# A norm chain for the first tile, products of zeros in the head, and two state-space parts three k-steps later

## The chip, the cores and the metric

One core of a Trainium2 chip runs the whole step. The metric is the device time of one execution in microseconds (us), as the median of several runs. Its engines are TensorE (PE: matmuls, and PEld for weight loads), VectorE (DVE), ScalarE (ACT), GpSimd (POOL) and SyncE (SP), which only issues transfers here. Each engine executes its own instructions in a fixed order and waits on semaphores for the others.

## The reference

One layer of a streaming encoder over 1024 prompt rows with 16 learned rows ahead of them, and 32 sample rows:

```
xn = rmsnorm(h);  z = xn @ w_in          # q latent | kv latent | rope key | u | g_a | g_b
o_a = attention(z) @ w_o_attn            # latent attention with rotary keys and a chunk mask
s   = gelu(y), y = s5_scan(u)            # 64 groups of 16 channels, 64 complex states each
        # x = f * (B u);  h_t = lam * h_{t-1} + x_t;  y = Re(C h) + D u
o_b = (s @ w_glu_v) * sigmoid(s @ w_glu_g)
h  += (sigmoid(g_a) * o_a + sigmoid(g_b) * o_b) @ w_out
h  += relu(rmsnorm(h) @ w_mlp_up)^2 @ w_mlp_down
```

The outputs are the rows, the new caches and the new states. Everything is float32 at the interface.

## The kernel before

Products run in float32r with both operands split into a high and a low half (`split`, L183 and L186): each 128x128 block is multiplied three times, xh·wh, xl·wh and xh·wl (`lin_part`, L261 to L271, the matmul is L267). ScalarE makes the high half by a copy, VectorE or POOL the low half by a subtraction. For the weights ScalarE makes `wh` and POOL `wl`, one unit ahead of its use.

**Head (L369 to L413).** A string, `HEAD`, lists the steps in order: `g` loads the norm's gains and spreads them over the partitions by two products (L393), `x` loads one of nine row tiles, `i` the identity, `l` and `w` load and split a weight unit, `n` with some digits computes the norm factors of these tiles in one chain (`stat`: a square with a row sum on ScalarE, L357, then ten small operations of `rsqrt` on VectorE), `m` scales a tile (L366), `t` transposes half a tile on TensorE and splits it into `xh` and `xl` (`to_cols`; tile 8 at once), and `p` runs one chunk of 268 columns of the first two weight units. `p00` is the first of these; it needs tiles 0, 1 and 8.

**State-space stage (about 37 to 440 us).** A loop over slots runs one unit of `w_in` in each (`run_unit`): 128 output columns, 8 k-steps of 9 matmuls, three products for three chunks of rows. The first slots compute units of u (chunks of 358 columns), later ones gates and latents (chunks of 396, 396 and 264 columns). These matmuls I call dense. Their PSUM tiles, tag `acc`, are five buffers, and a unit takes three; `finish` has ScalarE copy them to `gst` (L312, L314).

The state-space work comes in eight groups j of 128 channels, each in six parts that are laid over the slots by `START = [2, 4, 7, 9, 12, 15, 17, 20]`: `st0` in slot START[j], `st1` one slot later, `st2` two, `st3` four, `st4` five, `st5` six. A part that is a generator is advanced by one `next()` ahead of each k-step of the slot's unit (L263), so its TensorE work is mixed into the dense unit.

- `st0(j)`: POOL builds a table `tb` of powers by doubling (two memsets and 49 small operations, L554 to L562); VectorE builds `clm` and `wxt` (L419 to L427).
- `st1(j)`: TensorE transposes `wxt` (L584), ScalarE copies the result (L585); then the products `clm`·`bd` (L595) and `ext` (L602).
- `st2(j)`: TensorE computes the scan's input with U and W (L620), ScalarE copies it to `xs` (L626), VectorE multiplies with the table (A, Bt: L641, L642), adds (L643, L644), scans (L647), multiplies again (L649, L650) and forms `hb` (L653, L654). POOL makes the scan's coefficients L (L638 to L640).
- `st3(j)`: for four pairs of channel blocks TensorE multiplies U with M (L671) and adds `hb` times `clm` (L676); ScalarE copies to Y (L682); Y goes to DRAM and comes back as `yt`.
- `st4(j)`: the GELU's inner polynomial: square on ScalarE (L695), a multiply-add on VectorE (L696), `gw` on POOL (L697).
- `st5(j)`: tanh of `gw` on ScalarE (L702), the last product on VectorE (L703), and a store.

`tb` and `wxt` have one buffer each, `clm` two. After the stage come GLU, attention, the output projection and the MLP.

The program is written unit by unit, but the order on each engine is not the order of writing: the framework's scheduler places instructions by a simulated timeline of its own, so a step that is written later can move others that the diff doesn't touch.

Of the kernel before, what the change touches and what calls it, by code (L numbers as in the profile page):

```python
# [10 lines left out]
F32 = mybir.dt.float32  # L11
# [103 lines left out]
KENG = ['vpvpvpp', 'vvpppvv', 'vpvvvvv', 'vpppvpp']  # L115


HEAD = "g x0 x8 x1 i l0 x2 x3 l1 x4 x5 x6 x7 n081 m0 t00 m8 t01 t80 m1 t10 w t11 w p00 p01 n23 m2 t20 t21 m3 t30 t31 p10 p11 n4567 m4 t40 t41 m5 t50 t51 p20 p21 m6 t60 t61 m7 t70 t71 p30 p31"
CH0 = [(0, 268), (268, 268), (536, 268), (804, 268)]
START = [2 + int(2.6 * j) for j in range(8)]  # L120
G3 = [(0, 3), (3, 3), (6, 2)]
# [35 lines left out]
def tile_layer(ctx: ExitStack, tc: tile.TileContext, a: dict, o: list, dbg=None):  # L157
    nc = tc.nc
# [143 lines left out]
    with tc.tile_pool(reuse_waits="tile", name="s5", bufs=1) as sp, tc.tile_pool(reuse_waits="tile", name="sps", bufs=3, space=PSUM) as sps:  # L302
# [6 lines left out]
        def finish(kind, m, M, outs, st):  # L309
            for c0, n, ps in outs:  # L310
                if kind in "ab":
                    nc.scalar.activation(st[:M, c0:c0 + n], ps, AF.Tanh, scale=0.5)  # L312
                else:
                    nc.scalar.activation(st[:M, c0:c0 + n], ps, AF.Copy)  # L314
# [20 lines left out]
        X = {}  # L335
        spare = iter([("M", 2)] * 2 + [("U", 2)] * 2 + [("Y", 3)] * 3 + [("A", 1), ("Bt", 1)])

        def load_x(t):
            tag, bufs = next(spare)
            X[t] = sp.tile([128, D], F32, tag=tag, name="X", bufs=bufs)[:128 if t < 8 else 48]  # L340
            if t < 8:
                nc.sync.dma_start(X[t], x_p[t])
            else:
                nc.sync.dma_start(X[t][0:32], x_s)
                nc.sync.dma_start(X[t][32:48], a["meta_tokens"])
# [18 lines left out]
        def scale(t):  # L364
            R = X[t].shape[0]
            nc.vector.scalar_tensor_tensor(X[t], X[t], rsx[t], gbc[:R], op0=ALU.mult, op1=ALU.mult)  # L366
# [16 lines left out]

        for w in HEAD.split():
            op, i = w[0], [int(c) for c in w[1:]]
            if op == "g":

                grow = sp.tile([1, D + 128], F32, tag="clt", name="grow")
                nc.vector.memset(grow[:, D:], 1.0)
                nc.scalar.dma_start(grow[:, :D], a["norm_mix"])  # L390
                for q in range(2):
                    pt = sps.tile([128, 512], F32, tag="sp", name="sp")
                    nc.tensor.matmul(pt, lhsT=grow[:, D:], rhs=grow[:, 512 * q:512 * q + 512], start=True, stop=True)  # L393
                    nc.scalar.activation(gbc[:, 512 * q:512 * q + 512], pt, AF.Copy)
            elif op == "i":
                nc.sync.dma_start(ident, a["c_ident"])
            elif op == "x":
                load_x(*i)
            elif op == "l":
                ws.load(*i)  # L400
            elif op == "w":
                w01.append(ws.get(split_ahead=False))
            elif op == "n":
                stat(i)
            elif op == "m":
                scale(*i)
            elif op == "t":
                to_cols(*i)
            else:
                finish("u", i[1], 128, lin(gps, "acc", *w01[i[1]], *xfull, 8, 128, [CH0[i[0]]]), st01[i[1]])  # L410
# [3 lines left out]
        with ExitStack() as _:  # L414
# [91 lines left out]

            bb = sp.tile([128, 2, 32, 16], F32, tag="W", name="bb")
            for q, nme in enumerate(("ssm_b_re", "ssm_b_im")):
# [69 lines left out]
            def st1(j):  # L578
                cl, wx = hold[j]["cl"], hold[j]["wx"]
                W = sp.tile([128, 2, 4, 128], F32, tag="W", name="W")  # L580
                for q in range(2):
                    pp = sps.tile([128, 4, 128], F32, tag="sp", name="sp")
                    for g in range(4):
                        nc.tensor.transpose(pp[:, g], wx[:, q, g].rearrange("p a b -> p (a b)"), ident)  # L584
                    nc.scalar.activation(W[:, q], pp, AF.Copy)  # L585
                    yield

                for g2 in range(2):
                    hs = slice(64 * g2, 64 * g2 + 64)
                    for q in range(2):  # L590
                        V.tensor_copy(bd[hs, q, :, g2, :], bbar[hs, q, 4 * j:4 * j + 4])
                pk = sps.tile([128, 512], F32, tag="sp", name="sp")
                for g in range(4):
                    for q in range(2):
                        nc.tensor.matmul(  # L595
                            pk[32 * g:32 * g + 32, 0:128],
                            lhsT=bd[:, q, g].rearrange("p a b -> p (a b)"),
                            rhs=cl[:, q, g, 0:8].rearrange("p a b -> p (a b)"),
                            start=(q == 0), stop=(q == 1), tile_position=(0, 32 * g),
                        )  # L600
                yield
                V.tensor_copy(ext[:, 7:15].rearrange("p a b -> p (a b)"), pk[:, 0:128])  # L602
                V.scalar_tensor_tensor(ext[:, 7], m16, dd[:, j:j + 1], ext[:, 7], op0=ALU.mult, op1=ALU.add)
                nc.sync.dma_start(ext_d[j], ext.rearrange("p a b -> p (a b)"))
                M = sp.tile([128, 8, 128], F32, tag="M", name="M", bufs=2)
                src = ext_d[j].rearrange("(g c) x -> c g x", c=16)
                for s in range(T):
                    nc.sync.dma_start(M[16 * s:16 * s + 16], src[:, :, 16 * (7 - s):16 * (7 - s) + 128])
                hold[j].update(W=W, M=M)

            def st2(j):
                gs = slice(4 * j, 4 * j + 4)
                U, tb, W = hold[j]["U"], hold[j]["tb"], hold[j]["W"]
                G = nc.gpsimd

                for g in range(4):
                    px = sps.tile([128, 512], F32, tag="sp", name="sp")
                    for q in range(2):
                        for g2 in range(2):
                            nc.tensor.matmul(  # L620
                                px[64 * g2:64 * g2 + 64, KC * q:KC * q + KC],
                                lhsT=W[:, q, g, 64 * g2:64 * g2 + 64], rhs=U[:, 2 * g + g2],
                                start=True, stop=True, tile_position=(0, 64 * g2),
# [36 lines left out]
            def st3(j):  # L660
                hj = hold.pop(j)
                U, M, cl, hb = hj["U"], hj["M"], hj["cl"], hj["hb"]
                Y = sp.tile([128, 8, KQ], F32, tag="Y", name="Y", bufs=3)


                for ps_ in ((0, 1, 2), (3,)):
                    py = [sps.tile([128, 512], F32, tag="sp", name="sp") for _ in range(2)]
                    for e, pr in enumerate(ps_):
                        c = slice(e * KQ, (e + 1) * KQ)
                        for b in range(2):  # L670
                            nc.tensor.matmul(py[b][:, c], lhsT=M[:, 2 * pr + b], rhs=U[:, 2 * pr + b, 0:KQ],  # L671
                                             start=True, stop=False)
                        for q in range(2):
                            for b in range(2):
                                hs = slice(64 * b, 64 * b + 64)
                                nc.tensor.matmul(  # L676
                                    py[b][:, c], lhsT=cl[hs, q, pr, 1:9].rearrange("p a b -> p (a b)"),
                                    rhs=hb[hs, q, pr], start=False, stop=(q == 1),
                                )
                        yield  # L680
                    for b in range(2):
                        nc.scalar.activation(  # L682
                            Y[:, 2 * ps_[0] + b:2 * ps_[-1] + b + 1:2],
                            py[b][:, :len(ps_) * KQ].rearrange("p (g k) -> p g k", k=KQ), AF.Copy
                        )
                for g in range(8):
                    nc.sync.dma_start(y_d[j][16 * g:16 * g + 16].rearrange("c (t k) -> t c k", t=T), Y[:, g])
                yt = sp.tile([128, NQT], F32, tag="Y", name="yt", bufs=3)
                nc.sync.dma_start(yt, y_d[j])
                hold[j] = dict(yt=yt)  # L690

            def st4(j):
                yt = hold[j]["yt"]
                w = sp.tile([128, NQT], F32, tag="Y", name="gw", bufs=3)
                nc.scalar.activation(w, yt, AF.Square)  # L695
# [694 lines left out]
    with tc.tile_pool(reuse_waits="tile", name="mg", bufs=1) as mg:  # L1390
# [23 lines left out]
        for m in range(8):  # L1414
# [3 lines left out]
            for q in range(2):  # L1418
# [3 lines left out]
                pt = tpp.tile([128, 4, 128], F32, tag="tp", name="tp")  # L1422
# [5 lines left out]
            pt = tpp.tile([128, 512], F32, tag="tp", name="tp")  # L1428
# [21 lines left out]
    pt = tpp.tile([128, 512], F32, tag="tp", name="tp")  # L1450
# [8 lines left out]
    for g in range(3):  # L1459
        pt = tpp.tile([128, 512], F32, tag="tp", name="tp")  # L1460
        b = blk[4 * g:4 * g + 4]
        for c0, n in b:
            i = c0 // 128
            nc.tensor.matmul(pt[:, c0 - 512 * g:c0 - 512 * g + n], lhsT=y[:n, i:i + 1].to_broadcast([n, 128]),
                             rhs=ident[:n, :n], start=True, stop=True)
        w = sum(n for _, n in b)
# [109 lines left out]
```

## Time and profile before

| | us |
|---|---|
| median of 3 runs (2079.85 to 2081.4) | 2080.04 |
| the profiled execution | 2084.05 |
| its span | 2082.3 |
| TensorE busy | 2027.0 |
| VectorE busy | 1109.3 |
| ScalarE busy | 727.5 |
| POOL busy | 681.2 |

The mean granted clock of TensorE is 0.992 of full speed; full is 2.4 GHz, and the only other level is 1.2. A page of the profile shows one execution: busy times are sums of instruction durations, and the span runs from the first to the last instruction. In the timelines a number in square brackets is the time that the engine sat idle right before, with the instruction that released it.

### The profile page before, as it was taken

How to read it: one execution, taken by the hardware profiler on the slowest of the kernel's cores; microseconds unless marked ns; L12 is line 12 of the kernel's file. 1: busy time of each engine (PE TensorE's matmuls, PEld its weight loads, DVE VectorE, ACT ScalarE, POOL GpSimd, SP SyncE). 2: the span in 40 equal slices, each digit the busy share in tenths (PEclk: the TensorE clock that was granted, in tenths of full speed). 3: DMA queues.
4: the chain of work that ended last, by engine and by line, in shares of the span. 5: the costliest groups of instructions: out<-in, count | busy, mean ns of one | idle time of the engine just before them, and what ended most of it. 6: DMA issues, size and time to landing. Idle time of an engine off the chain costs nothing.

```text
span 2082.3 us, 34103 instructions
## 1 busy us (share of the span) xinstructions
PE 2027.0 (97%) x12943; PEld 1923.2 (92%) x12943; DVE 1109.3 (53%) x3048; ACT 727.5 (35%) x1738; POOL 681.2 (33%) x916
## 2 busy tenths in 40 slices
PE   6999999999999899999999999999999999999999
PEld 6988888899999788888888999999999999999999
DVE  5969776534575688888885544432222222222222
ACT  4213222223332567676755223321222212122222
POOL 0577776621222334233444211112121221212121
PEclk9999999999999999999999999999999999999999
DMA  5334434435444101110114434411111121211113
GB/s 144 113 109 124 137 117 143 134 119 173 134 129 129 44 5 28 17 28 17 26 23 132 150 119 125 171 31 56 36 51 50 37 58 35 61 31 56 41 41 104
DMA packets 256177, 170.70 MB, mean 82 GB/s; under 512 B 63240, under 2 KB 239453, under 8 KB 256014
## 3 DMA queue, kind: packets, MB, share of 16 engines
q1 hardware_dynamic: 256012, 168.53, 27.7%
q8 instruction: 102, 1.67, 0.3%
q14 instruction: 61, 0.50, 0.1%
q10 hardware_dynamic: 2, 0.00, 0.0%
HBM read 124.08 MB, written 44.41 MB: 81 GB/s over the span
## 4 chain that ended last, share of the span: by engine, by line
PE 82%; DVE 12%; DMA 2%; ACT 2%; issue 1%; POOL 0%; SPq 0%; ACTq 0%; DVEq 0%; POOLq 0%
PE acc L267 40%; PE pj L267 22%; PE po L1274 3%; PE pj L1045 3%; PE pj L1105 2%; PE pt L1249 1%; PE sp L676 1%; PE Sp L1192 1%; PE Sp L1184 1%; PE Sp L1187 1%; PE Sp L1185 1%; PE Sp L1186 1%; DVE clt L419 1%; PE sp L620 1%; PE sp L671 1%
## 5 line engine op out<-in xcount | busy, mean ns | idle before, releaser
L186 POOL TENSOR_TENSOR wl<-raw,wh 128x1024 fp32r<-128x1024 f32 (+2 forms) x164 | 331.3, 2021 | 981.8 <-ACT wh L183 971.9
L183 ACT ACTIVATE wh<-raw 128x1024 fp32r<-128x1024 f32 (+2 forms) x166 | 148.8, 896 | 755.9 <-PE acc L267 354.2
L267 PE MATMUL acc<-xh,wh 128*128 128x264 f32 (+6 forms) x736 | 188.9, 337 | 1.8 <-ACT xh L183 1.8
L267 PE MATMUL acc<-xh,wl 128*128 128x264 f32 (+4 forms) x736 | 181.2, 327 | 0.0
L267 PE MATMUL acc<-xl,wh 128*128 128x264 f32 (+5 forms) x736 | 181.0, 327 | 0.0
L267 PEld LDWEIGHTS acc<-xh,wh 128*128 128x128 f32 (+1 forms) x736 | 127.4, 190 | 14.3 <-issue 7.4
L267 PEld LDWEIGHTS acc<-xl,wh 128*128 128x128 f32 (+1 forms) x736 | 129.6, 190 | 2.1 <-issue 0.7
L267 PEld LDWEIGHTS acc<-xh,wl 128*128 128x128 f32 (+1 forms) x736 | 129.7, 190 | 1.8 <-issue 0.7
L1501 DVE TENSOR_TENSOR yacc<-pj,yacc 128x352 f32<-128x352 f32 x96 | 44.5, 518 | 139.5 <-PE pj L267 139.5
L1501 DVE TENSOR_TENSOR yacc<-acc,yacc 128x352 f32<-128x352 f32 (+1 forms) x96 | 44.6, 518 | 113.0 <-PE acc L267 113.0
L186 DVE TENSOR_TENSOR al<-t,ah 128x352 fp32r<-128x352 f32 x96 | 64.7, 700 | 71.6 <-ACT ah L183 71.6
L267 PE MATMUL acc<-sh,wh 128*128 128x352 f32 x384 | 93.0, 325 | 1.0 <-ACT sh L751 1.0
L267 PE MATMUL acc<-sl,wh 128*128 128x352 f32 x384 | 93.6, 324 | 0.0
L267 PE MATMUL acc<-sh,wl 128*128 128x352 f32 x384 | 92.9, 324 | 0.0
L1483 DVE SCALAR_TENSOR_TENSOR t<-acc,rstd 128x352 f32<-128x352 f32 x48 | 23.5, 518 | 117.9 <-PE acc L267 117.9
L267 PE MATMUL acc<-ah,wl 128*128 128x352 f32 (+1 forms) x384 | 85.2, 324 | 0.0
L267 PE MATMUL pj<-al,wh 128*128 128x352 f32 x384 | 84.6, 324 | 0.0
L267 PE MATMUL pj<-ah,wh 128*128 128x352 f32 x384 | 84.3, 323 | 0.0
L267 PE MATMUL acc<-al,wh 128*128 128x352 f32 (+1 forms) x384 | 84.1, 323 | 0.0
L267 PE MATMUL acc<-ah,wh 128*128 128x352 f32 (+1 forms) x384 | 84.0, 323 | 0.0
L267 PE MATMUL pj<-ah,wl 128*128 128x352 f32 x384 | 84.0, 323 | 0.0
L267 PE MATMUL acc<-ha,wh 128*128 128x352 f32 x360 | 77.5, 323 | 4.1 <-ACT mh__13991 L183 4.1
(468 smaller groups left out, 5388.6 us busy)
## 6 DMA issues: line engine op xcount, KB each, us to landing
raw<-in_w_mlp_up_dram SPq DMA_DIRECT2D x32, 512.0 KB
raw<-in_w_mlp_down_dram SPq DMA_DIRECT2D x64, 256.0 KB
raw<-in_w_in_dram SPq DMA_DIRECT2D x29, 512.0 KB
ud<-gst SPq DMA_DIRECT2D x8, 536.0 KB
U<-ud SPq DMA_DIRECT2D x64, 67.0 KB
yd<-Y SPq DMA_DIRECT2D x64, 66.0 KB
yt<-yd SPq DMA_DIRECT2D x8, 528.0 KB
sd<-gw SPq DMA_DIRECT2D x8, 528.0 KB
```

The source lines that it names most:

```text
L183: nc.scalar.activation(hi, src, AF.Copy)
L186: lo_eng.tensor_tensor(lo, src, hi.bitcast(F32), ALU.subtract)
L267: nc.tensor.matmul(pt[:M, :n], lhsT=w[:, k, :], rhs=x(k, c0, n), start=(k == 0 and p == 0), stop=(k == kt - 1 and p == 2),)
L419: eng.tensor_tensor(t1, ar, br, ALU.mult)
L620: nc.tensor.matmul(px[64 * g2:64 * g2 + 64, KC * q:KC * q + KC], lhsT=W[:, q, g, 64 * g2:64 * g2 + 64], rhs=U[:, 2 * g + g2], start=True, ...
L671: nc.tensor.matmul(py[b][:, c], lhsT=M[:, 2 * pr + b], rhs=U[:, 2 * pr + b, 0:KQ], start=True, stop=False)
L676: nc.tensor.matmul(py[b][:, c], lhsT=cl[hs, q, pr, 1:9].rearrange("p a b -> p (a b)"), rhs=hb[hs, q, pr], start=False, stop=(q == 1),)
L1045: nc.tensor.matmul(ps[:R], lhsT=x[:, c, k0:k0 + R], rhs=w[:, c, :], start=(c == 0 and q == 0), stop=(c == 1 and q == 2))
L1105: nc.tensor.matmul(ps[:R, :384], lhsT=x[:, c, 128 * i:128 * i + R], rhs=w[:, c, :], start=(c == 0 and q == 0), stop=(c == 2 and q == 2))
L1274: nc.tensor.matmul(po[:, :256], lhsT=w, rhs=x, start=st["first"], stop=(last and q == len(grp) - 1))
L1483: nc.vector.scalar_tensor_tensor(t, ps, 0.0, rstd[:, c], op0=ALU.max, op1=ALU.mult)
L1501: nc.vector.tensor_tensor(yacc[:, m, c], ps, yacc[:, m, c], ALU.add)
```

## The change

Three edits.

1. In the head tile 0 has a norm chain of its own, and is scaled and transposed ahead of tiles 8 and 1, which share one. The identity's load is issued before x1's.
2. After the gain products a tile `zero` is set to zero on VectorE, and five products of 512 columns of it go to a PSUM tile that nothing reads. `zero` uses the buffer of `tb`, which is not yet in use.
3. `st1` and `st3` begin with three empty yields, so their work starts three k-steps later in the unit that they are mixed into.

```diff
-HEAD = "g x0 x8 x1 i l0 x2 x3 l1 x4 x5 x6 x7 n081 m0 t00 m8 t01 t80 m1 t10 w t11 w p00 p01 n23 m2 ...
+HEAD = "g x0 x8 i x1 l0 x2 x3 l1 x4 x5 x6 x7 n0 m0 t00 t01 n81 m8 m1 t80 w t10 t11 w p00 p01 n23 m2 ...
...
                     nc.scalar.activation(gbc[:, 512 * q:512 * q + 512], pt, AF.Copy)
+
+                zero = sp.tile([128, 1088], F32, tag="tb", name="zero")
+                nc.vector.memset(zero, 0.0)
+                pt = sps.tile([128, 512], F32, tag="sp", name="sp")
+                for q in range(5):
+                    nc.tensor.matmul(pt, lhsT=zero[:, 0:128], rhs=zero[:, 0:512], start=(q == 0), stop=(q == 4))
...
             def st1(j):
                 cl, wx = hold[j]["cl"], hold[j]["wx"]
                 W = sp.tile([128, 2, 4, 128], F32, tag="W", name="W")
+                for _ in range(3):
+                    yield
...
                 Y = sp.tile([128, 8, KQ], F32, tag="Y", name="Y", bufs=3)
+                for _ in range(3):
+                    yield
```

Lines of the changed kernel lie 6 higher than those named above from L395 on, 8 higher behind `st1`'s yields, 10 higher behind `st3`'s.

**TensorE in slot 6**, where `st3(0)` and `st2(1)` are mixed into a unit of u. Before, the first products with M and `hb` stand ahead of the unit's first matmul:

```order
L267 MATMUL acc<-xh,wl 128x356
L671 MATMUL sp<-U,M 128x132 x2
L676 MATMUL sp<-hb,clm 128x132 x4
L620 MATMUL sp<-U,W 64x134 x4
L267 MATMUL acc<-xh,wh 128x358 x2
```

Now it begins with the scan's input, and so it goes on:

```order
L628 MATMUL sp<-U,W 64x134 x4
L267 MATMUL acc<-xh,wh 128x358 x2
L267 MATMUL acc<-xl,wh 128x358 x2
L267 MATMUL acc<-xh,wl 128x358 x2
L628 MATMUL sp<-U,W 64x134 x4
```

The first use of `hb` moved behind 27 dense matmuls and 12 of the scan's input.

**VectorE around the polynomial of `st4(0)`** (L696 before, L706 now). Before, it stands between the two scans of group 1:

```order
L647 SCALAR_TENSOR_TENSOR Gs<-L,A 128x544
L696 TENSOR_SCALAR gw<-gw 128x1056
L647 SCALAR_TENSOR_TENSOR Gs<-L,A 128x544
L419 TENSOR_TENSOR clt<-pw,bbar 128x128
L420 TENSOR_TENSOR clt<-pw,bbar 128x128
L421 TENSOR_TENSOR wxt<-clt 128x8x16 x3
L649 TENSOR_TENSOR A<-Gs,tb 128x1088
L650 TENSOR_TENSOR Bt<-Gs,tb 128x1088
```

Now it comes after that group's `hb` and after `clm` of group 2:

```order
L661 TENSOR_TENSOR hb<-A,Bt 128x4x128
L662 TENSOR_TENSOR hb<-A,Bt 128x4x128
L661 TENSOR_TENSOR hb<-A,Bt 128x4x4
L662 TENSOR_TENSOR hb<-A,Bt 128x4x4
L664 TENSOR_TENSOR fin<-A,Bt 128x8
L665 TENSOR_TENSOR fin<-A,Bt 128x8
L431 SCALAR_TENSOR_TENSOR clm<-clt 128x144 x4
L706 TENSOR_SCALAR gw<-gw 128x1056
L425 TENSOR_TENSOR clt<-pw,bbar 128x128
```

The scans and both products with the table moved ahead of it as well.

**POOL from the end of table 1 on.** Before, the weights' `wl` and `gw(0)` follow the table (1233), and the next table (1801) begins behind them:

```order
L427 TENSOR_TENSOR tb_1233<-tt_1234 128x4x3
L186 TENSOR_TENSOR wl_1906<-raw_1607,wh_1905 128x1024
L697 TENSOR_TENSOR gw_1788<-gw_1788,yt_1722 128x1056
L638 COPY L_2360<-mg8_779 128x544
L554 MEMSET tb_1801 128x4
L555 MEMSET tb_1801 128x4
```

Now the next table (1822) begins first:

```order
L433 TENSOR_TENSOR tb_1254<-tt_1255 128x4x3
L646 COPY L_2381<-mg8_800 128x544
L186 TENSOR_TENSOR wl_1927<-raw_1628,wh_1926 128x1024
L647 MEMSET L_2381 128x4
L648 MEMSET L_2381 128x4
L560 MEMSET tb_1822 128x4
L561 MEMSET tb_1822 128x4
```

and `gw(0)` comes 17 operations later:

```order
L428 TENSOR_TENSOR tt_1823<-tb_1822,ek_804 128x4x4
L429 TENSOR_TENSOR tt_1823<-tb_1822,ek_804 128x4x4
L707 TENSOR_TENSOR gw_1809<-gw_1809,yt_1794 128x1056
L433 TENSOR_TENSOR tb_1822<-tt_1823 128x4x4
L425 TENSOR_TENSOR tt_1823<-tb_1822,ek_804 128x4x8
```

The same trade of places happens at tables 4 and 7. ScalarE's order around `tanh(0)` is the same in both: table load, tanh, one `wh`, then the three copies of slot 7's unit to `gst`. On TensorE the third chunk of slot 8's unit comes, in the new order, after two chunks of three k-steps and five products of `st3(1)`.

## Rows read from the trace of the kernel before

**Rows 1.** The page, part 1: busy time, share of the span and instructions of each engine.

```profile
PE 2027.0 (97%) x12943; PEld 1923.2 (92%) x12943; DVE 1109.3 (53%) x3048; ACT 727.5 (35%) x1738; POOL 681.2 (33%) x916
```

**Rows 2.** TensorE's waits by releaser, 0 to 60 us, then 60 to 440 us (total, times, longest).

```profile
PE sp L372 <- DVE X L366: 9.1, 1, 9.1
...
PE sp L584 <- DVE wxt L421: 5.5, 4, 2.2
PE sp L676 <- DVE hb L653: 4.2, 2, 4.0
```

**Rows 3.** Timeline of TensorE, state-space stage: start, duration, operation, [idle before <- releaser].

```profile
133.35 1.25 PE L676 MATMUL sp<-hb,clm 64*128 64x132 f32 x8 [3.98 <-DVE hb L653]
...
169.66 0.33 PE L584 MATMUL sp<-ident,wxt 128*128 128x128 f32 x1 [0.85 <-DVE wxt L421]
...
253.90 0.33 PE L584 MATMUL sp<-ident,wxt 128*128 128x128 f32 x1 [2.21 <-DVE wxt L421]
...
385.62 0.33 PE L584 MATMUL sp<-ident,wxt 128*128 128x128 f32 x1 [1.91 <-DVE wxt L421]
```

**Rows 4.** Windows: us, busy (x) of PE, PEld, DVE, ACT, POOL, PEclk, DMA share, GB/s.

```profile
120.00:140.00 20.00, 16.02 (x94) 14.74 (x94) 13.04 (x22) 2.65 (x7) 12.51 (x37) 0.83 0.23 59
254.40:257.80 3.40, 3.40 (x13) 3.38 (x12) 3.40 (x12) 0.46 (x1) 3.35 (x4) 0.50 0.23 93
21.70:25.70 4.00, 4.00 (x16) 3.77 (x17) 3.51 (x12) 1.45 (x3) 0.00 (x0) 1.00 0.63 64
26.69:28.67 1.98, 1.98 (x18) 1.98 (x17) 1.64 (x11) 0.15 (x1) 0.00 (x0) 1.00 0.22 40
131.40:136.45 5.05, 3.10 (x19) 2.51 (x20) 2.27 (x11) 0.52 (x3) 4.23 (x17) 0.51 0.08 26
169.70:178.26 8.56, 8.51 (x65) 7.55 (x66) 6.92 (x27) 1.60 (x4) 7.88 (x17) 1.00 0.32 128
```

**Rows 5.** Timelines of TensorE and ScalarE in the head, 0 to 36 us.

```profile
2.25 3.75 PE L393 MATMUL sp<-grow 1*128 1x512 f32 x4 [2.25 <-DMA grow<-in_norm_mix_dram]
...
21.68 0.82 PE L267 MATMUL acc<-xh,wh 128*128 128x268 f32 x2 [0.39 <-ACT xh L183]
...
16.29 0.60 ACT L183 ACTIVATE xh<-sp 128x512 fp32r<-128x512 f32 x1 [0.15 <-PE sp L372]
16.78 1.05 ACT L357 ACTIVATE sq<-X 128x1024 f32<-128x1024 f32 x1
```

**Rows 6.** Timeline of TensorE, slots 6 to 8.

```profile
149.16 0.68 PE L620 MATMUL sp<-U,W 128*64 128x134 f32 x8
...
156.11 0.53 PE L267 MATMUL acc<-xh,wh 128*128 128x396 f32 x2
...
167.87 0.61 PE L671 MATMUL sp<-U,M 128*128 128x132 f32 x4
```

**Rows 7.** Timeline of VectorE, slot 7.

```profile
149.27 1.15 DVE L421 TENSOR_TENSOR clm<-clt 128x144 f32<-128x144 f32 x4 [15.57 <-PE sp L676]
...
151.94 1.28 DVE L641 TENSOR_TENSOR A<-xs,tb 128x1088 f32<-128x1088 f32 x1
...
158.06 1.28 DVE L647 TENSOR_TENSOR_SCAN Gs<-L,A 128x544 f32<-128x544 f32 x1
159.26 0.68 DVE L696 TENSOR_SCALAR gw<-gw 128x1056 f32<-128x1056 f32 x1
...
161.06 2.41 DVE L419 TENSOR_TENSOR clt<-pw,bbar 128x128 f32<-128x128 f32 x1
```

**Rows 8.** Timeline of ScalarE, slots 7 and 8.

```profile
165.83 1.09 ACT L702 ACTIVATE gw<-gw 128x1056 f32<-128x1056 f32 x1 [4.13 <-POOL gw L697]
...
168.59 1.15 ACT L312 ACTIVATE gst<-acc 128x396 f32<-128x396 f32 x3
```

**Rows 9.** Timeline of POOL, slots 7 and 8.

```profile
163.29 2.51 POOL L697 TENSOR_TENSOR gw<-gw,yt 128x1056 f32<-128x1056 f32 x1
...
169.71 3.57 POOL L419 TENSOR_TENSOR tt<-tb,ek 128x4 f32<-128x4 f32 x1
```

More of the change, by code (lines that the diff above doesn't have):

```diff
@@ L115 @@
 KENG = ['vpvpvpp', 'vvpppvv', 'vpvvvvv', 'vpppvpp']
-HEAD = "g x0 x8 x1 i l0 x2 x3 l1 x4 x5 x6 x7 n081 m0 t00 m8 t01 t80 m1 t10 w t11 w p00 p01 n23 m2 t20 t21 m3 t30 t31 p10 p11 n4567 m4 t40 t41 m5 t50 t51 p20 p21 m6 t60 t61 m7 t70 t71 p30 p31"
+HEAD = "g x0 x8 i x1 l0 x2 x3 l1 x4 x5 x6 x7 n0 m0 t00 t01 n81 m8 m1 t80 w t10 t11 w p00 p01 n23 m2 t20 t21 m3 t30 t31 p10 p11 n4567 m4 t40 t41 m5 t50 t51 p20 p21 m6 t60 t61 m7 t70 t71 p30 p31"
 CH0 = [(0, 268), (268, 268), (536, 268), (804, 268)]
```

## The prediction

> **What bounds the kernel.** The page's first part comes first: TensorE is busy 97% of the span, VectorE 53% [rows 1], so the bound is TensorE. No edit here takes matmuls out of a busy stretch; it can only remove idle time, or time at the low clock. TensorE's table of waits says where that is: the head, 9.1 us for the first scaled tile, and the state-space stage, 5.5 us on `wxt` in four stalls and 4.2 on `hb` in two between 60 and 440 us [rows 2]. The timeline places them: 3.98 us on `hb` at 133.35 in slot 6, then on `wxt` 0.85 in slot 8, 2.21 in slot 13 and 1.91 in slot 21 [rows 3]; what is left of the sums is 0.5 on `wxt` (slot 3) and 0.2 on `hb` (slot 16). Two are longer than they look. TensorE's clock is granted at 0.83 between 120 and 140 us, and at 0.50 (1.2 GHz) from 254.4 to 257.8, just after the stalls of slots 6 and 13 [rows 4]. At half clock half of the time is lost: 1.7 us at slot 13; at slot 6 the mean of 0.83 over 20 us is 3.4 us, of which I count 2.5, the rest lying in the stall.
>
> So all the state-space stage can give back is 5.5 + 4.2 of waits and 4.2 at the low clock, 13.9 us, 0.7% of the time. One measurement can tell some 0.2%, 4.2 us, from no change.
>
> **The change, part by part.** The sum is made against the profiled execution, 2084.05 us (span 2082.3), 4.0 us over the median of 2080.04; I move the difference to the median.
>
> *Head.* A chain of its own has x0 scaled before x8 and x1 are. It costs VectorE one norm chain more, ten small operations in 1.98 us [rows 4]. But the first product p00, now at 21.68, needs x8 and x1 as well, and on ScalarE one more square (1.06 us, as X4's) stands ahead of the first copy: 16.29 now, 17.4 then [rows 5]. VectorE does all of the old work and one chain more before p00, ScalarE just the old, so p00 stays near 21.7 (21.6 to 22.4), and the scalings of the later tiles move by the added chain at most. I take +0.4, bounds −2 and +1.5.
>
> *Products of zeros.* The memset is one VectorE pass over 1088 columns, 1.28 by the nearest row [rows 7], while VectorE waits for the squares. Two gain products took 3.75 us, so five take 9.4, from 6.0 to 15.4 at worst [rows 5], less if the clock rises on the way. TensorE is idle for 9.1 us there [rows 2], and nothing reads the result. Without this cover x0's transposes would move from 12 to 15.4, still ahead of the copy at 17.4. Cost 0.
>
> By the Trainium skill (TensorE: Matmul & The Clock Gate, "The HAM clock gate") a busy array is granted its full clock and an idle one half, so the zeros would have p00 run at full rate; by that rule p00 would gain some 2 us. The trace agrees that p00 starts slowly behind idle time, though its granted clock is shown as 1.00: 16 products in 4.00 us from 21.7, then 18 in 1.98 [rows 4]. But in the new order too TensorE idles right before p00, from about 15 to 17.4.
>
> *st3 three k-steps later, slot 6.* 27 dense matmuls and 12 of the input projection now stand ahead of the first use of `hb(0)`: 27 × 0.163 (slot 7's 72 products take 156.11 to 167.87) + 12 × 0.17 (eight passes, four products, in 0.68) = 6.4 us [rows 6] against a stall of 3.98. The stall goes, and the low clock after it: −6.5. st1's delay puts 4 × 0.16 or more ahead of the transposes in slot 3: −0.54; the 0.23 of slot 16 goes too. Slot 8's `wxt` stall of 0.85 goes by the 27 matmuls.
>
> *What is late next, slot 8.* With these 7.0 us gone TensorE opens slot 8 at 167.87 − 7.0 = 160.9. Then 18 products of 396 columns, at 0.163 × 396/352 = 0.183, are 3.3 us and five small ones 0.6 [rows 6]: at 164.8 it wants the third column chunk. This chunk's PSUM buffer is the first of slot 7's unit, one of five, and its copy out on ScalarE stands behind `tanh(0)` and one `wh` split, both before and after. Before, tanh ran at 165.83 once POOL's `gw(0)` was done, and the copies at 168.59, in time [rows 8]. Now `gw(0)` is later twice: on VectorE its polynomial stands behind group 1's whole scan part, on POOL behind 17 operations of the next table, which wait for the last reader of `tb(1)`. The chain, with durations from [rows 7 to 9]:
> - POOL's table 1 was ready for VectorE's first product with it at 151.94, and is about 1 us earlier now that less delays POOL's start: the two products, 1.28 each, end near 153.
> - Two sums of half the size 1.3, two scans 2.5: 156.8. Four `clm` 1.1: 157.9. Two products 2.6, one of them held by POOL's `wl` as the small product of 161.06 was (2.41 where its like take 0.29), 2.1: 162.6. This frees POOL's table.
> - VectorE goes on: eight small products and four `clm` at 0.29 are 3.4, `hb` (two of half size) 1.3, then the polynomial 0.7: 168.0.
> - POOL from 162.6: 17 small operations. Undisturbed the same 17 of table 1 took 5.05 us (131.40 to 136.45); beside a busy VectorE the first of table 2 alone was held 3.57, and fifteen of them took 8.56 (the row's 17 count a memset and the next operation) [rows 4, 9]. I take 8.6: 171.2. `gw` 2.5: 173.7.
> - ScalarE: tanh 1.1, `wh` 1.0 (165.83 to 168.59 held both, and a wait of 0.7), first copy 0.4: 176.2.
>
> TensorE waits 164.8 to 176.2, **11.4 us**. Without contention the table is free at 160.5, the 17 operations end at 165.5, the polynomial at 165.9, `gw` at 168.4 and the copy at 170.9: a wait of 6.1. I take 11.4 since the row at 169.71 is the same operation of the same table at the same place beside the same engine. After a wait of that length the low clock comes back; the row of slot 13 prices it at 1.7, that of slot 6 at 2.5: +2.0.
>
> By the Trainium skill (SBUF — State Buffer, "Who interferes with whom") the two engines share one port pair that the later one waits for until the running instruction ends; POOL would then lose one VectorE operation, at most 1.3 us, at its first product, and the wait would be some 2 us less. The row shows 3.57 us, longer than any of VectorE's operations then (0.28 to 1.28).
>
> *Slots 13 and 21.* POOL's order repeats with tables 4 and 7 (`gw(2)` and `gw(5)` behind the next table's first operations). Their start is less sure, so I take the undisturbed 6.1 each, and the low clock of 1.7 for slot 13. Removed are 2.21 + 1.7 and 1.91.
>
> **Sum:** head +0.4; slot 3 −0.5; slot 6 −6.5; slot 8 −0.85 + 11.4 + 2.0 = +12.55; slot 13 6.1 + 1.7 − 3.9 = +3.9; slot 16 −0.2; slot 21 6.1 − 1.9 = +4.2. Together +13.85: 2097.9 for a profiled execution, **2093.9** on the median's footing.
>
> Elsewhere nothing moves: the order after the stage's end is as before. GLU reads what the last parts write, 27 products or 4.4 us later for group 7; the projection units that follow them without state-space parts cover it, and without that cover it costs 4.4.
>
> **Rivals.**
> 1. *No new wait (faster).* Place: the first copy of slot 7's unit on ScalarE. If `gw(0)` leaves POOL before about 162, so that tanh, `wh` and the copy end by 164.8, TensorE never asks in vain, and only the removed stalls count: −0.5 − 6.5 − 0.85 − 3.9 − 0.2 − 1.9 + 0.4 = −13.5, 2066.5; with a wait of a few us at the three places, 2071. For it: ScalarE was in time before, and no row of TensorE's waits in the stage names `gst` [rows 2]. Against: `gw` stands behind a chain that even undisturbed ends at 168.4. Chance 0.25, since a chain of twelve links can be off by its first.
> 2. *Gains and waits cancel (same).* The undisturbed chain: slot 8 −0.85 + 6.1, slots 13 and 21 waiting about as long as they did, slot 6 −6.5, slot 3 −0.5, slot 16 −0.2, head +0.4: −1.6, 2078.4, give or take 4. For it: durations on POOL are rough. Chance 0.15.
> 3. *The zeros do what their name says*: p00 at full rate from its start saves about half of the 4.00 us that its first 16 products take at 0.25 each, where later ones take 0.11 [rows 4]: −2 us. That is worth something only if VectorE had the later tiles scaled early too, and it has one chain more to do. Chance 0.1 inside any of the cases; it would give 2091.9.
> 4. The forecast, waits of 6 to 12 us in slot 8 and some at the other two: 0.6. With 12 at all three it would be 2110.
>
> **The numbers.** Predicted 2094. The range 2072 to 2101 takes in the cancelling case and the edge of the first rival, and above it 8 us for more contention in slots 13 and 21; below it are 0.13, above 0.07. The likeliest case alone lies at 2085 to 2103. Faster by over 0.2%: 0.25, all of rival 1; within: 0.15; slower: 0.6.
>
> **What would show it.** TensorE's row in slot 6 has no wait on `hb`, and the granted clock of 120 to 140 is 1.0; in slots 8, 13 and 21 it waits for ScalarE's `gst`, with a lower clock behind, ScalarE's tanh waits for POOL's `gw`, and POOL's `gw` comes after the first operations of the next table. p00 starts at 21.6 to 22.4. The prediction is wrong if no wait on `gst` of over 4 us is in these slots.

## The result, and the profile after

The changed kernel takes 2100.17 us (median of four runs, 2095.48 to 2102.9) where the kernel before took 2080.72 beside it (2079.85 to 2084.93): a ratio of 1.0067 [1.005, 1.0085]. By the ratio it is slower by 0.67%, some 14 us; the two medians themselves are 19.5 us apart. The time lies inside the forecast's range (2072 to 2101) and close to its upper end. The profiled execution took 2101.14 us with a span of 2099.4, 17.1 over the span before. Page of the changed kernel, part 1:

```profile
PE 2040.3 (97%) x12953; PEld 1930.4 (92%) x12953; DVE 1100.5 (52%) x3058; ACT 729.1 (35%) x1738; POOL 701.0 (33%) x916
```

Against [rows 1], TensorE has ten more instructions (the five products of zeros are recorded as ten) and 13.3 us more busy time, 7.5 of them the zeros in what was idle time of the head. So it isn't work that came in the state-space stage; part of what came is idle time, and part is the same work at a lower clock. The changed kernel's table of TensorE's waits, 60 to 470 us (total, times, longest), shows the first:

```profile
PE acc L267 <- ACT gst L312: 17.9, 3, 11.0
PE sp L628 <- DVE ext L610: 1.7, 1, 1.7
PE acc L267 <- POOL wl L186: 1.3, 1, 1.3
```

The waits on `wxt` and `hb` of [rows 2] are gone, all of them: 9.7 us. In their place stand 20.9 us, 17.9 of them on ScalarE's copy to `gst`, in three places. The timeline of TensorE has them, with the two small ones (start, duration, operation, [idle before <- releaser]; the lines of the state-space code are six to ten further down than before):

```profile
130.33 0.67 PE L628 MATMUL sp<-U,W 128*64 128x134 f32 x6 [1.66 <-DVE ext L610]
...
163.65 0.63 PE L267 MATMUL acc<-xh,wl 128*128 128x396 f32 x2 [1.25 <-POOL wl L186]
...
178.62 0.59 PE L267 MATMUL acc<-xh,wh 128*128 128x264 f32 x1 [11.04 <-ACT gst L312]
...
265.26 0.59 PE L267 MATMUL acc<-xh,wh 128*128 128x264 f32 x1 [3.22 <-ACT gst L312]
...
399.45 0.59 PE L267 MATMUL acc<-xh,wh 128*128 128x264 f32 x1 [3.61 <-ACT gst L312]
```

These are slots 6, 8 (twice), 13 and 21, the slots of [rows 3]. The second part shows in windows behind each stall and in the head (us, busy (x) of PE, PEld, DVE, ACT, POOL, then PEclk, DMA share, GB/s):

```profile
131.90:135.30 3.40, 3.40 (x12) 2.72 (x11) 0.00 (x0) 0.52 (x3) 2.77 (x15) 0.50 0.38 96
178.60:183.00 4.40, 4.38 (x17) 3.90 (x18) 4.37 (x10) 0.85 (x3) 4.17 (x7) 0.50 0.62 248
265.30:271.80 6.50, 6.50 (x24) 6.02 (x25) 6.04 (x9) 1.18 (x3) 6.26 (x9) 0.50 0.21 86
399.50:404.90 5.40, 5.40 (x20) 4.93 (x21) 1.04 (x1) 1.17 (x3) 5.24 (x7) 0.50 0.55 210
20.80:24.80 4.00, 3.94 (x16) 3.62 (x17) 3.83 (x14) 1.47 (x3) 0.00 (x0) 0.50 0.97 168
700.00:1140.00 440.00, 421.32 (x2665) 363.95 (x2664) 370.11 (x1496) 285.60 (x860) 170.29 (x281) 0.97 0.14 31
```

PEclk is 0.50, 1.2 GHz, in each of the four stretches behind a stall. Half of such a stretch is lost: 1.7, 2.2, 3.3 and 2.7 us, 9.9 together, against 4.2 before.

**Where the 11.04 us come from.** Three timelines of the changed kernel, slots 7 and 8, read from the end backwards. ScalarE:

```profile
156.00 1.28 ACT L712 ACT_TABLE_LOAD   x1
176.16 1.08 ACT L712 ACTIVATE gw<-gw 128x1056 f32<-128x1056 f32 x1 [18.87 <-POOL gw L707]
177.15 1.04 ACT L183 ACTIVATE wh<-raw 128x1024 fp32r<-128x1024 f32 x1
178.09 1.15 ACT L312 ACTIVATE gst<-acc 128x396 f32<-128x396 f32 x3
```

ScalarE does nothing for 18.87 us. The three copies that TensorE wants stand in its queue behind a `wh` split and a tanh, and the tanh waits for POOL's `gw`. POOL:

```profile
154.56 6.67 POOL L646 COPY L<-mg 128x544 f32<-128x544 f32 x1 [5.31 <-DVE Gs L655]
161.19 2.40 POOL L186 TENSOR_TENSOR wl<-raw,wh 128x1024 fp32r<-128x1024 f32 x1
...
163.79 6.12 POOL L425 TENSOR_TENSOR tt<-tb,ek 128x4 f32<-128x4 f32 x1
169.86 0.20 POOL L426 TENSOR_TENSOR tt<-tb,ek 128x4 f32<-128x4 f32 x1
...
173.72 2.41 POOL L707 TENSOR_TENSOR gw<-gw,yt 128x1056 f32<-128x1056 f32 x1
```

`gw` comes behind the first 17 operations of the next table, as the order said. Their first, on four elements a partition, is held for 6.12 us; the other 16 take 3.9. Ahead of them a copy of 544 columns is held for 6.67, and POOL's `wl` behind it is late for TensorE: the 1.25 us at 163.65. VectorE at the same time:

```profile
155.27 1.28 DVE L657 TENSOR_TENSOR A<-Gs,tb 128x1088 f32<-128x1088 f32 x1
156.47 1.28 DVE L658 TENSOR_TENSOR Bt<-Gs,tb 128x1088 f32<-128x1088 f32 x1
...
161.27 2.35 DVE L664 TENSOR_TENSOR fin<-A,Bt 128x8 f32<-128x8 f32 x1
...
164.50 0.70 DVE L706 TENSOR_SCALAR gw<-gw 128x1056 f32<-128x1056 f32 x1
...
169.16 0.68 DVE L433 TENSOR_TENSOR wxt<-clt 128x128 f32<-128x128 f32 x3
```

The table is free at 157.75, the polynomial is done at 165.2; VectorE runs its small operations one behind the other to 169.8, which is when POOL's held one comes through at last. So in slot 8 there are two delays of the same size: VectorE began the polynomial 8.5 us after ScalarE's square of its input (done at 155.99), and POOL began `gw` 8.5 us after the polynomial.

In slots 13 and 21 POOL's order is the same, but the table costs little: `gw` began 1.2 us after the polynomial was done. What is late there is the polynomial, which VectorE began 4.4 and 6.0 us after ScalarE's square of its input. VectorE and POOL in slot 13:

```profile
258.38 0.70 DVE L706 TENSOR_SCALAR gw<-gw 128x1056 f32<-128x1056 f32 x1
260.30 2.47 POOL L707 TENSOR_TENSOR gw<-gw,yt 128x1056 f32<-128x1056 f32 x1
```

**The sum as measured**, step by step. Slot 3: −0.5. Slot 6: the stall of 3.98 became one of 1.66 and the low clock's 2.5 became 1.7, −3.1. Slot 8: −0.85 + 11.04 + 1.25 + 2.2 = +13.6. Slot 13: 3.22 + 3.3 − 3.9 = +2.6. Slot 16: −0.2. Slot 21: 3.61 + 2.7 − 1.9 = +4.4. Together +16.8. The stage itself, from group 0's first `sp<-U,W` product to the first product of GLU (`acc<-sh`), took 99.04 to 496.70 before and 95.85 to 509.52 now. That is 397.7 and 413.7 us, +16.0. Of the span's +17.1 the other +1.1 is −3.2 ahead of the stage and +4.3 behind it, where the order of the instructions is the same in both kernels; the granted clock of 700 to 1140 us is 0.97 here and 0.99 in the record before. Neither can be laid on the change: that first product starts anywhere from 95.4 to 99.0 us in the records of this study, in no order by their heads, and the stretch behind the stage varies too (last section). So I compare the stage's length, and the time by ratios.

### The profile page after: what moved, and what is told of

Same layout as the page of the kernel before. It is cut to its first block, busy times and chain, and to the rows that moved or that the text cites. A ratio compares the mean times of both kernels' runs of the same rounds, so it can differ in the third digit from the quotient of the medians.

```text
span 2099.4 us, 34132 instructions
## 1 busy us (share of the span) xinstructions
PE 2040.3 (97%) x12953; PEld 1930.4 (92%) x12953; DVE 1100.5 (52%) x3058; ACT 729.1 (35%) x1738; POOL 701.0 (33%) x916
## 4 chain that ended last, share of the span: by engine, by line
PE 78%; DVE 10%; POOL 5%; DMA 2%; ACT 2%; issue 2%; SPq 0%; POOLq 0%; ACTq 0%; DVEq 0%
PE acc L267 37%; PE pj L267 22%; PE pj L1055 3%; PE po L1284 3%; PE pj L1115 2%; PE pt L1259 1%; PE Sp L1202 1%; PE Sp L1194 1%; POOL tt L425 1%; PE Sp L1197 1%; PE Sp L1195 1%; PE Sp L1196 1%; POOL tt L428 1%; PE sp L686 1%; POOL tb L427 1%
## 5 line engine op out<-in xcount | busy, mean ns | idle before, releaser
L186 POOL TENSOR_TENSOR wl<-raw,wh 128x1024 fp32r<-128x1024 f32 (+2 forms) x164 | 345.3, 2106 | 953.1 <-ACT wh L183 943.0
L267 PE MATMUL acc<-xh,wh 128*128 128x264 f32 (+6 forms) x736 | 192.0, 341 | 19.6 <-ACT gst L312 17.9
L267 PE MATMUL acc<-xh,wl 128*128 128x264 f32 (+3 forms) x736 | 182.4, 328 | 1.3 <-POOL wl L186 1.3
L267 PE MATMUL acc<-xl,wh 128*128 128x264 f32 (+4 forms) x736 | 183.2, 329 | 0.1
```

The costliest lines, as they stand in the source:

```text
L186: lo_eng.tensor_tensor(lo, src, hi.bitcast(F32), ALU.subtract)
L267: nc.tensor.matmul(pt[:M, :n], lhsT=w[:, k, :], rhs=x(k, c0, n), start=(k == 0 and p == 0), stop=(k == kt - 1 and p == 2),)
```

## The experiments

My theory: the whole loss is `gw` behind the next table on POOL, which holds the tanh, which holds the copies. Rivals: the loss comes from another part of the change (the head, `st1`'s yields), or from TensorE meeting some other late producer, whatever ScalarE does. Every kernel below does all of the computation. The stage's length is that from the first `sp<-U,W` to the first `acc<-sh` product in each one's profile (397.7 before).

**One part of the change at a time.** *e1_head* has the new head and the products of zeros alone:

```
-HEAD = "g x0 x8 x1 i l0 ... t00 m8 t01 t80 m1 ..."
+HEAD = "g x0 x8 i x1 l0 ... n0 m0 t00 t01 n81 m8 m1 t80 w ..."
+                zero = sp.tile([128, 1088], F32, tag="tb", name="zero")
...
```

> Only the head's two edits (norm chain of tile 0, products of zeros); both state-space parts start as before. Theory (the loss is the late tanh in slots 8, 13 and 21, which st3's delay makes): no wait of TensorE on gst, the stalls of before on hb (4 us) and wxt (5.5 us) are back, and the head is some 2.4 us shorter, so 2078 us, 2 to 3 below before. Rival (the head's edits shift the clock or the weights' transfers for the rest of the program): 2085 or more.

Measured: 2085.34 us, 1.0009 [0.9997, 1.0021], stage 396.5. The time is in the rival's range, but the kernel before took 2084.26 beside it. The `wxt` and `hb` waits are back (4.0 and 3.1 us, where the kernel before has 5.5 and 4.2), and there is none on `gst`. So the head costs nothing that can be told, and it gives nothing either; the gain that the theory had here isn't there.

*e3_st1* has only `st1`'s three yields, *e4_st3* only those of `st3`:

```
+                for _ in range(3):
+                    yield
```

> Only st1 three k-steps later. Theory: no wait on gst over 1 us, since POOL's order of gw and the next table is as before; the wxt stalls of slots 3, 8, 13 and 21 (5.5 us) go, the hb stall of slot 6 (4 us) stays: 2076 us, 3 to 6 below before. Rival (the later wxt work is what pushes gw and tanh back): waits on gst of 3 us and more in these slots, 2085 or more.

Measured: 2086.34 us, 1.0019 [1.0007, 1.0031], stage 401.5: a miss. All `wxt` waits are gone, as expected, but the table of waits has other ones in their place:

```profile
PE sp L678 <- DVE hb L655: 10.3, 4, 4.8
PE acc L267 <- ACT gst L312: 0.6, 1, 0.6
```

`wxt` and `hb` come from the same queue on VectorE. A TensorE that no longer stops for the one arrives earlier at the other, which isn't ready sooner: counted from the stage's start, every group's `hb` is done 0.2 to 4.3 us later than in the kernel before. The rival, waits on `gst`, falls too.

> Only st3 three k-steps later. Theory: waits on gst of about 11, 3 and 3.5 us in slots 8, 13 and 21, as in the change, with the low clock behind them, and no hb stall in slot 6: 2095 to 2102 us. Rival (both delays together make the wait): under 2088, waits on gst under 6 us in all.

Measured: 2114.32 us, 1.0155 [1.0134, 1.0176], stage 427.3. `st3`'s yields alone are slower, as the theory says, but by more than it says, and without its waits: of the 11, 3 and 3.5 us on `gst` only one of 5.4 is there, in slot 8. That much of the rival holds, though not its time:

```profile
PE sp L584 <- DVE wxt L421: 12.5, 6, 6.7
PE acc L267 <- ACT gst L312: 5.4, 1, 5.4
PE sp L584 <- DVE wxt L427: 4.7, 2, 2.9
PE acc L267 <- POOL wl L186: 3.6, 1, 3.6
```

In slot 8 the tanh starts at 176.11 there, in the changed kernel at 176.16: the late `gw` comes with `st3`'s yields. TensorE only asks for the copy later, held up before it by `wl` and `wxt`. In all it spends 17 us on `wxt`, since `st1`, not moved, asks for it early. With `st3` late, `st1`'s delay is worth 427.3 − 413.7 = 13.6 us; on its own it is worth nothing.

*e5_delay1* has one yield in both places in place of three.

> The change with one empty yield in place of three in st1 and st3. In this kernel POOL still has gw(0) ahead of the next table, and gw(3) only three table operations into it. Theory (the loss comes with the trade of places on POOL and VectorE, not with each k-step): no wait on gst over 3 us, the hb stall of slot 6 half gone, 2080 to 2087 us. Rival (each k-step of delay costs its share): a third of the change's loss, waits on gst of some 4 us in slot 8, 2088 to 2092.

Measured: 2091.39 us, 1.0045 [1.0029, 1.0061], stage 408.3. The theory's expectation fell, and the time is the rival's. In slot 8 the wait on `gst` is only 0.30, but slots 13 and 21 have 4.65 and 4.79, and VectorE's waits are back in part, 7.2 us on `hb` and 2.6 on `wxt`.

The rival's share doesn't hold either: a third of the delay costs two thirds of the stage's loss (10.6 of 16.0 us), and not in slot 8, where it put the wait. In slots 13 and 21 `gw` stands behind only three of the table's operations, but begins 5.7 and 4.8 us after the polynomial is done, since POOL's operations ahead of it are held again (in slot 13 the copy of 544 columns, for 7.16 us).

**Taking the chain apart.** *e7_gw_dve* is the changed kernel with `gw`'s first product on VectorE, so that no table of POOL's can stand ahead of it:

```
-                nc.gpsimd.tensor_tensor(w, w, yt, ALU.mult)
+                V.tensor_tensor(w, w, yt, ALU.mult)
```

> The change with one operation moved: gw, the polynomial's product of st4, runs on VectorE instead of POOL, so tanh no longer waits for POOL's 17 table operations. Theory (POOL's queue holds gw): in slot 8 gw is done by about 168, tanh and the copy to gst by 171, so the wait of 11 us falls to 2 to 4 and those of slots 13 and 21 to under 1.5: 2082 to 2088 us, 12 to 18 below the change. Rival (VectorE's own order is what makes gw late): waits on gst of 8 us or more in slot 8, 2095 or more.

Measured: 2086.39 us, 1.0015 [1.0003, 1.0027], stage 402.2. The tanh starts 7 us earlier, and TensorE's wait in slot 8 falls from 11.04 to 2.90; slot 21 has 0.69, but slot 13 has 4.91, more than the expected 1.5: VectorE does the polynomial only at 254.03 there and `gw` at 255.56, and no table has a part in that. Another 3.86 us on `wl` at 100.81 stand ahead of the first `gw`. ScalarE and POOL of this kernel, slot 8:

```profile
169.21 1.08 ACT L712 ACTIVATE gw<-gw 128x1056 f32<-128x1056 f32 x1 [10.08 <-DVE gw L707]
...
171.15 1.15 ACT L312 ACTIVATE gst<-acc 128x396 f32<-128x396 f32 x3
```

```profile
155.74 6.67 POOL L646 COPY L<-mg 128x544 f32<-128x544 f32 x1 [5.32 <-DVE Gs L655]
...
164.98 8.66 POOL L425 TENSOR_TENSOR tt<-tb,ek 128x4 f32<-128x4 f32 x1
173.59 0.20 POOL L426 TENSOR_TENSOR tt<-tb,ek 128x4 f32<-128x4 f32 x1
```

The table's first operation is held even longer, 8.66 us, and it no longer matters.

*e8_tanh_last* leaves `gw` on POOL, late as it is, and puts the tanh behind the copies: its bias is a zero made from the last column that the unit before copied.

```
+            lastst[0] = st
...
-                nc.scalar.activation(w, w, AF.Tanh)
+                zb = sp.tile([128, 1], F32, tag="zb", name="zb", bufs=2)
+                nc.scalar.activation(zb, lastst[0][:, NQT - 1:NQT], AF.Copy, scale=0.0)
+                nc.scalar.activation(w, w, AF.Tanh, bias=zb)
```

> The change with tanh made to read a zero taken from the last copied column of the unit before (one 128x1 operation more on ScalarE per group), so that it can only come behind that unit's three copies to gst. Theory (gw is late, and whatever stands behind tanh on ScalarE is late with it): the waits on gst go, and TensorE waits instead for the copies of W or Y that still stand behind tanh, 6 to 9 us in slot 8; 2088 to 2098. Rival (only the place of tanh ahead of the three copies costs the time): no wait over 3 us in slots 8, 13 and 21; 2080 to 2086.

Measured: 2080.51 us, 0.9984 [0.997, 0.9998], stage 397.1. That is below what I expected and in the rival's range, though the rival has no wait over 3 us and one of 4.33 is there: I had thought that TensorE would lose more on the next thing behind the tanh. ScalarE of this kernel:

```profile
162.12 1.18 ACT L312 ACTIVATE gst<-acc 128x396 f32<-128x396 f32 x3
163.33 0.20 ACT L715 ACTIVATE zb<-gst 128x1 f32<-128x1 f32 x1
176.76 1.18 ACT L716 ACTIVATE gw<-gw,zb 128x1056 f32<-128x1056 f32 x1 [13.23 <-POOL gw L709]
177.84 0.58 ACT L595 ACTIVATE W<-sp 128x512 f32<-128x512 f32 x1
```

The tanh is as late as in the changed kernel (176.76), the copies 16 us earlier, and no wait on `gst` is left. TensorE does meet the next thing, `W`, also behind the tanh, but only for 4.33 us at 178.47. This run decides the cause: the lateness of `gw` costs time only through what stands behind the tanh, and almost all of that is the three copies. It takes off all that the change cost, 413.7 to 397.1.

*e10_gw_tanh* has both edits.

> Both: gw on VectorE and tanh behind the three copies. Theory: no wait on gst, waits on W or Y under 3 us in slot 8, so all the stalls of before are gone: 2078 to 2084. Rival (VectorE's chain is the next limit in slots 8, 13 and 21): waits on wxt, hb or wl of 8 us and more in all, 2086 or more.

Measured: 2079.72 us, 0.9981 [0.9972, 0.9991], stage 395.4. The time is as expected, and hardly better than that of the kernel before or e8. Slots 8, 13 and 21 have no wait on `gst`, `W` or `Y`, but not all stalls are gone: 8.2 us of waits are left, 3.3 of them on `gst` at 207.88, where the copies stand behind ScalarE's square of group 1. So the delays give back some 2 us of the 13.9 that were to be had.

**A better kernel.** *e11_before_gw* is the kernel before with e7's one line.

> The kernel before with gw on VectorE, nothing else. Theory (POOL's large products slow VectorE's small ones around slots 8, 13 and 21): VectorE gets 1.3 us more per group but loses no time to gw, the wxt stalls of 5.0 us in these slots shrink by 1 to 3 us: 2078 to 2084, up to 4 below before. Rival (VectorE is the limit there, and any work more on it lengthens the stalls): the wxt stalls grow by 1 us each, 2086 to 2089.

Measured: 2072.82 us, 0.9947 [0.993, 0.9964], stage 389.2: faster than both kernels, and more than expected. TensorE's waits of 60 to 470 us, and the window of the same stretch (columns as above):

```profile
PE sp L676 <- DVE hb L653: 4.4, 2, 4.0
PE sp L584 <- DVE wxt L421: 1.4, 3, 0.6
```

```profile
60.00:470.00 410.00, 404.24 (x2749) 374.26 (x2748) 269.68 (x682) 107.61 (x265) 237.73 (x457) 1.00 0.44 128
```

The stalls on `wxt` fell from 5.5 to 1.4 us though VectorE has an operation more, and the low clock behind slot 13 went with them. The tanh of slot 8 starts at 163.23 there, 165.83 before [rows 8]. POOL is busy 24.4 us less in this stretch than before (262.10), which is what the eight products that moved took there (24.8); on VectorE they take 10.0. The theory shows in a product of VectorE's that ran beside POOL's `gw` (163.29 to 165.80) before, and no longer does (before, then e11):

```profile
163.40 2.55 DVE L420 TENSOR_TENSOR clt<-pw,bbar 128x128 f32<-128x128 f32 x1
160.70 0.72 DVE L420 TENSOR_TENSOR clt<-pw,bbar 128x128 f32<-128x128 f32 x1
```

Of the 8.5 us of the stage, 3.9 are waits and some 2.5 low clock (1.7 behind slot 13, 0.8 behind slot 6); the rest isn't placed.

Three more try to add to it. *e13_gw_head* adds the change's head and zeros:

> The kernel before with gw on VectorE and with the head's two edits. Theory (the head's edits are worth nothing, the differences between profiles in the head are of the run): within 2 us of the version without them, 2071 to 2075. Rival (they save 2 to 3 us, as the head of the first profile after looked): 2069 to 2071.

Measured: 2077.87 us, 0.9962 [0.9948, 0.9977], stage 389.2, the same as e11 to a tenth. The time is above the expected range, but the kernel before took 2085.07 beside it, and the intervals of the ratios overlap; the head is worth nothing here that can be told.

*e12_gw_j0* delays `st3` for group 0 alone, to take out the one stall that e11 still has:

```
+                for _ in range(3 if j == 0 else 0):
+                    yield
```

> The kernel before with gw on VectorE, and st3 three k-steps later for group 0 alone, to take the hb stall of slot 6 (4.0 us and the low clock after it) out of the best version so far. Theory (what slot 6 gives back, slot 8 takes, since VectorE's and ScalarE's order there flips as in the change): no hb stall in slot 6, and in slot 8 new waits on gst, wxt or wl of 3 to 8 us; 2070 to 2077, no better than without this edit by more than 3 us. Rival (with gw on VectorE the flip is harmless): no wait over 1 us in slot 8, 2064 to 2068.

Measured: 2086.61 us, 1.0002 [0.9989, 1.0014], stage 396.9. Slot 6 has no stall on `hb` any more, and slot 8 has this one:

```profile
170.45 0.45 PE L584 MATMUL sp<-ident,wxt 128*128 128x128 f32 x1 [6.27 <-DVE wxt L421]
```

VectorE reached the `wxt` after group 1's `hb`, its `clm` and the polynomial. What slot 6 gains, slot 8 loses, and more: by the ratios this is 0.55% above e11, some 11 us, where I expected some 4 at most.

*e16_gw_j0_tanh* puts the tanh of e12 behind the copies.

> The first of these three, and tanh made to come behind the copies of the unit before. Theory (behind tanh the copies are what stalls TensorE): the wait on gst in slot 8 goes, what is left in slot 8 is a wait on wxt or W under 4 us, and slot 6 stays without the hb stall: 2066 to 2073. Rival (tanh later makes the stored result and W later in slots 11, 13, 16 and so on): new waits of 3 us and more there, 2075 or more.

Measured: 2087.03 us, 1.0006 [0.9991, 1.002], stage 399.6: a miss. e12 has no wait on `gst` in slot 8 that could go, and its 6.27 us on `wxt` stand there unchanged; the rival has the time but not the waits, the new ones are 1.0 to 1.5 us. That stall is the order of VectorE's own queue, and ScalarE has no part in it.

## Why the prediction was right

**Direction and mechanism: right, with slot 8 as the place that shows all of it.** The wait on `gst` in slots 8, 13 and 21, the tanh behind POOL's `gw`, `gw` behind the next table, and the lower clock behind each stall all are in the profile. e8 and e7 show that it is the cause: each breaks the chain at another link, and each takes off most of the 16.0 us that the stage lost (16.6 and 11.5). In slots 13 and 21 the table adds only 1.2 us; what `gw` waits for there is the polynomial, late on VectorE. The forecast's price for these two slots was of that kind: its undisturbed chain has the table's operations done at 165.5 and the polynomial at 165.9.

**The total: in part luck.** The sum was +13.85 for a measured +16.8. Slot 6 was off by 3.4, slot 8 by 1.05 and slot 21 by 0.2, and slot 13 by −1.3 and the head by −0.4 the other way.

**Slot 8: +12.55 forecast, +13.6 measured.** The wait was 11.04 for 11.4, but both of its ends lie later than worked out: TensorE asked at 167.6, not 164.8, since slot 6 gave back less and `wl` cost 1.25; the copy came at 178.5, not 176.2. Inside the chain two errors cancel. The table was free at 157.75 and not at 162.6: I had `wl` hold one of the two products, and it held the small `fin` at 161.27 (2.35 us), behind them. POOL's 17 operations, though, began only at 163.79, behind the held copy and `wl`, and then took 9.9 for 8.6.

**The row against the rule.** I priced POOL's first operation by the row that showed 3.57 us [rows 9]. It took 6.12. By the Trainium skill (SBUF — State Buffer, "Who interferes with whom") it waits until the instruction that runs on VectorE ends; the trace doesn't agree, since VectorE began and ended more than twenty operations in that time.

**Slot 6: −6.5 forecast, −3.1 measured.** The wait on `hb` went, as the sum has it. The step that failed is "the stall goes, and the low clock after it": a new wait came a few products earlier. The `U`,`W` products need the PSUM tile that `ext` (L610) reads, and that copy stands on VectorE behind group 0's `hb`. It is 1.66 us, and the clock fell after it all the same: from 120 to 140 us it was granted at 0.91, not at the 1.0 that the forecast names.

**Slots 13 and 21: +3.9 and +4.2 forecast, +2.6 and +4.4 measured.** Terms mis-sized both ways. The waits were 3.22 and 3.61 for 6.1 each, the low clock cost 3.3 and 2.7 for 1.7 and nothing. These tables' first operations were not held (0.26 us at 249.68 and at 383.87). After a stall the time at the low clock doesn't follow the stall's length: 4.4 us behind 11.04 (where the clock had fallen at 169.4, inside the stall), 6.5 behind 3.22.

**Head: +0.4 forecast, nothing measured.** p00 starts at 20.80, against 21.68 in [rows 5], but kernels with the old head started it between 20.5 and 21.7 and those with the new one between 20.3 and 21.5. e1 and e13 give it no time in either direction. The start came earlier than the 21.6 to 22.4 that the forecast names, but not by more than the kernels differ. Rival 3 falls, though the zeros did raise the clock: their ten records start 0.85 us apart up to 11.8 and 0.43 apart from 12.5 on. But at 19.2 the clock fell to 0.50, and p00 ran its first 4.0 us at that. Its pace is the one before: 16 products in 3.94 us here, in 4.00 us there, where [rows 4] show a clock of 1.00 that doesn't fit it (nor does the 1.00 shown for the first of the zeros). Between the zeros and p00 TensorE did little; its timeline, and windows as above:

```profile
6.54 7.46 PE L400 MATMUL sp<-zero 128*128 128x512 f32 x10
13.83 1.04 PE L372 MATMUL sp<-ident,X 128*128 128x128 f32 x8
20.80 0.81 PE L267 MATMUL acc<-xh,wh 128*128 128x268 f32 x2 [0.38 <-ACT xh L183]
```

```profile
14.00:19.20 5.20, 2.10 (x20) 1.62 (x18) 5.17 (x9) 4.86 (x9) 0.14 (x2) 1.00 1.10 332
19.20:20.80 1.60, 1.21 (x6) 0.72 (x5) 1.24 (x5) 1.60 (x5) 0.00 (x0) 0.51 1.61 88
```

By the Trainium skill (TensorE: Matmul & The Clock Gate, "The HAM clock gate") an idle array goes back to half clock; the trace agrees, with an array that was idle for the larger part: busy 2.10 of 5.20 us, then a clock of 0.51 and 0.50. Zeros that run up to the first product were not tried.

**Rivals 1 and 2** fall with the wait of 11.04. e8 and e10 show what rival 1 would have been, had the copies been in time: not 2066.5 but close to the time before, 0.998 of it. Its sum took every removed stall for a gain, where e3 and e12 show that VectorE's next product is late in its place.

## What to carry to other kernels

Where an order is fixed for each engine, look at what stands behind an instruction that waits for another engine: here three copies that had nothing to do with the tanh held TensorE for 17.9 us. A part that is moved later to clear a stall clears it only if its producer's queue has slack; on a queue that is late by itself (VectorE in e3, e4 and e12) the stall comes back at the next product. Take work off the pair of engines that hold each other up instead: one product moved from POOL to VectorE took 0.53% off the kernel before, more than any reordering here.

## What the runs showed of the hardware

- POOL's small operations were held far beyond one VectorE instruction: 6.12 and 8.66 us for four elements a partition, 6.67 us for a copy of 544 columns that takes 1.76 in slot 13, while VectorE ran back to back.
- The granted clock fell to 0.50 behind a stall of 1.66 us, and stayed there 6.5 us behind one of 3.22 but 4.4 us behind one of 11.04. Behind the stall of 4.0 us on `hb`, with the same instructions, it was 0.50 for 5.0 us in the record before and for 3.4 us in e11's.
- The stretch from 700 to 1140 us, whose order is the same in all of these kernels, has a granted clock of 0.97 in the changed kernel's record, 0.99 in that of the kernel before and of e11; the attention stretch in it took between 431 and 439 us over the thirteen records. With differences of some microseconds, the length of the stage tells kernels apart where the total doesn't.
